# Two-layer retention and convolution trunk on one Trainium2 core: last key tile over 128 rows, TensorE and ScalarE in source order, weight splits one step behind their sums

## Chip, core and metric

The kernel runs on one core of one Trainium2 chip. The metric is the device time of one execution in microseconds (us). Three runs of the kernel before gave 1560.03, 1561.87 and 1566.96; the median is 1561.87. The engines are named PE (TensorE; PEld is its weight load), ACT (ScalarE), DVE (VectorE), POOL (GpSimd) and SP (SyncE, which issues the DMAs).

## What is computed

The reference is a trunk of two layers over 16 + 512 = 528 tokens and 1024 channels. Cut to what matters:

```
for l in range(2):
    xn = rmsnorm(h, pre_norm_g[l])
    proj = xn @ w_in[l] + b_in[l]                # 1024 x 12288
    c_h,c_b,c_c,c_z, r_q,r_k,r_v,r_z, g_a,g_b = split(proj)
    y_a = (c_b * conv3(c_c * c_h) * silu(c_z)) @ w_conv_out[l]
    y_b = (groupnorm(retention(rope(r_q), rope(r_k), r_v)) * silu(r_z)) @ w_ret_out[l]   # 4 heads
    y = (sigmoid(g_a) * y_a + sigmoid(g_b) * y_b) @ w_o[l]
    h = h + rmsnorm(y, post_norm_g[l])
return h[:, 16:]
```

## The kernel before

**Precision.** Every product of a weight and an activation is made of three matmuls on reduced fp32 (fp32r): high part by high part, high by low, low by high. So every weight tile is split: a cast to the high part on ACT (L142) and the difference on DVE (L143), together `split`. Raw weights come by DMA from SP into `raw` tiles; the pairs of split weights are `whi`/`wlo` (four slots) and `whd`/`wld`.

**A Group** (class `Group`) computes 256 output channels for all tokens with seven multiplications of block sums in place of eight (Strassen's scheme). Each multiplication, `mul` (L279), is 12 matmuls of up to 264 columns into one PSUM bank, and between multiplications ACT reads a bank out (`put` at L325, the copy from `pb` to `pa` at L335). In the order of the source these are M1 (bank `pb`, then ACT copies `pb` to `pa`), M5 (`pc`), the pending last multiplication of the group before, S2 (`pb`), A12 (`pa`), S4 (`pc`), S3 (`pb`); the group's own last one, A22, is left in `pending`, accumulates onto the same `pb` bank that S3 used, and is entered by `close()`, either inside the next group or ahead of a `RetOut`. A22 may start only when ACT's `put` has read S3 from that bank. The weights of S2 to S4 and A22 are sums of raw blocks, made on DVE (L307, L314, L315) ahead of their split.

**Between groups** stand `RetOut` (the retention output, L244, two rounds of 48 matmuls; its run begins with `close()`), `ConvOut` (also L244), the retention itself (scores L425, transposes L450, `attend` L484), and at the layer boundary `wo_half`, `norms` and `opening` (L678; norm statistics L370, spread over partitions L384 with ACT's copy L387). The end is the output projection on token rows (L1167) with its own norm (L1183, L1188).

**The retention's last key tile** has 64 keys which lie twice in 128 rows. Its scores are split into `Shi` (128 rows) and `Slo`; in `attend` the pass with `Slo` multiplies the first 64 rows alone.

**What sets the order.** The source calls `tick()` after each multiplication, and `later(n, fn)` puts work n ticks behind; evictions are marked with high priority. A scheduler then orders the instructions of each engine, so a row of PE need not stand where the source has it: it moves matmuls whose inputs are ready in between others. SP, POOL and DVE are ordered in the same way.

Of the kernel before, what the change touches and what calls it, by code (L numbers as in the profile page):

```python
# [11 lines left out]
F32 = mybir.dt.float32  # L12
# [3 lines left out]
ALU = mybir.AluOpType  # L16
# [40 lines left out]
def trunk(ctx: ExitStack, tc: tile.TileContext, xT, w_in, binT, w_co, w_ro, w_o, gpre, gpost,  # L57
# [104 lines left out]
    def load(fn):  # L162
# [3 lines left out]
        return order[0]  # L166

    def prep(kind, need, frees, fn, ready=lambda: True):
        preps.append((kind, need, frees, fn, ready))
# [30 lines left out]
    def pair_of(ref, dram):  # L200

        need = plain_load(ref, dram)

        def go():
            ref["w"] = wtile("whi"), wtile("wlo")
            split(*ref["w"], ref["raw"])
        prep("pair", need, 1, go)
# [76 lines left out]
    class Group:  # L284
        def __init__(self, l, col, i0, cb, act=AF.Identity):
# [6 lines left out]
            prep("one", need[2], 0, self.last)  # L292
            self.raw, self.w = [None] * 3, [None] * 4

# [9 lines left out]
        def halves(self, j):  # L304
            if j != 1:
                r = self.raw[j]
                nc.vector.tensor_tensor(r[:, 512:], r[:, 512:], r[:, 0:512], op=ALU.add)  # L307
            self.w[j] = wtile("whi"), wtile("wlo")
            split(*self.w[j], self.raw[j])

# [7 lines left out]
        def last(self):  # L318
            self.w[3] = tuple(wsd.tile([P, 512], F32R, tag=x, name=nm(x)) for x in ("whd", "wld"))
            split(*self.w[3], self.t4)  # L320

# [5 lines left out]
        def run(self, s1_first=False):  # L327
            l, m, n, w = self.l, self.m, self.n, self.w
            t1, t2, s = fslot(), fslot(), fslot()
            b, c = bank("pb"), bank("pc")  # L330

            def m1():
# [10 lines left out]
            used("pair")  # L343
            close()
            mul(b, S2, w[1], 0, n, False)
            self.put(s, 0, b, scale=-1.0)
            mul(pa, A12, w[1], 1, n, False)
            self.put(t1, 0, pa, self.act)
            used("pair")
            mul(c, S4, w[2], 0, n, False)  # L350
            self.put(t2, 0, c, bias=bias(l, m + 1))
# [5 lines left out]

            def end():
                mul(b, A22, w[3], 0, n, False)
                self.put(t1, 1, b, self.act, bias=bias(l, m))  # L360
# [54 lines left out]
    def scores(l, q, k, k8, Shi, Slo, js):  # L415
# [14 lines left out]
        for n, j, cols in todo:  # L430
# [10 lines left out]
            ss = slice(SOFF[j] + o, SOFF[j] + o + cols.w)  # L441
            later(1, lambda kn=kn, ss=ss, sv=sv: split(Shi[0:kn, ss], Slo[0:kn, ss], sv))

# [22 lines left out]
    def attend(l, h, Shi, Slo, V, v, t, sums):  # L466
# [12 lines left out]
        for n, (j, x, y, b, lo_, hi_) in enumerate(todo):  # L479
            _, kn, q0 = JT[j]  # L480
            if j == len(JT) - 1 and x == 0:
                kn = CHUNK
            S = (Shi, Slo)[y]
# [44 lines left out]
    class RetOut:  # L528
# [4 lines left out]
        def run(self, yr):  # L533
            cols = QCOLS[self.l]
            close()
            for mm in range(2):
                i = self.q * 2 + mm
# [74 lines left out]
    class ConvOut:  # L612
# [6 lines left out]
        def run(self, conv, ga):  # L619
            cols = QCOLS[self.l]  # L620
            cs = slice(cols.t0, T)
            pp = pslot()
            hi, lo = (kview(x, KD) for x in self.ref["w"])
            mm_tile([pp[:, 0, :], pp[:, 1, :]], hi, lo, slice(0, P), lambda k: conv[k][0], lambda k: conv[k][1], KD, cols)
# [147 lines left out]
    def norms(l, half, hts, ysum, hsum, R2, R):  # L772
# [22 lines left out]
        later(2, lambda: tok("y", ysum))  # L795
        later(5, lambda: spread(R2, st["y"], half * HALF, 88, 3))
        for k in range(KD):
            later(5, lambda k=k: resid(k))
        later(13, lambda: tok("h", hsum))
        later(16, lambda: spread(R, st["h"], half * HALF, 88, 3))  # L800
        for k in range(KD):
            later(16, lambda k=k: scaled(k))

# [22 lines left out]
    for l in range(DEPTH):  # L826
# [35 lines left out]
        def q_done(ts, hd, h, l, d=8):  # L862
# [4 lines left out]
            def tables():  # L867
                hd["S"] = [gr.tile([P, SW], F32R, tag="S", name=nm(x), bufs=2) for x in ("Shi", "Slo")]
                nc.sync.dma_start(Dsb, decay[h])
            later(3, tables)  # L870
# [205 lines left out]
    for l in range(DEPTH):  # L1076
# [74 lines left out]
        else:  # L1151
# [62 lines left out]
            for t in range(2, SEQ // P):  # L1214
                st = state()
                for half in range(2):
                    o = pslot()[:, 0, :]
                    for k in range(KD):
# [86 lines left out]
```

## Time and profile before

| | before |
|---|---|
| median of three runs | 1561.87 us |
| profiled execution | 1560.22 us, of which the span 1558.4 us |
| PE busy | 1537.1 us (99%) |
| PEld busy | 1487.0 us (95%) |
| DVE busy | 1166.1 us (75%) |
| ACT busy | 912.2 us (59%) |
| POOL busy | 18.8 us (1%) |
| granted TensorE clock, mean of the span | 1.000 |

Busy time on PE has modelled ends, since matmuls are pipelined. Where PE waits is therefore read from the starts: consecutive matmuls of 264 columns start about 0.12 us apart, and a longer distance between two starts is time lost. The figure in brackets at a row's end is the idle time of the engine ahead of it by the profile, with what ended it.

### The profile page before, as it was taken

What the parts mean: (1) busy time and instruction counts of PE and PEld (TensorE: products, weight loads), DVE (VectorE), ACT (ScalarE), POOL (GpSimd) and SP (SyncE); (2) the same over time, 40 slices, a digit from 0 to 9 for tenths busy, and PEclk for the clock granted to TensorE, in tenths of its full rate; (3) what the DMA queues carried; (4) which work ended last, traced back from release to release, by engine and by line L of the source; (5) the groups of instructions that cost most, each with busy time, mean ns of one, the idle gap of its engine ahead of it and who ended that gap; (6) DMA issues with size and microseconds to landing.
All of it is one profiled execution on the core that took longest, in us unless ns stands there. A gap on an engine that the chain in (4) does not pass through costs nothing.

```text
span 1558.4 us, 29296 instructions
## 1 busy us (share of the span) xinstructions
PE 1537.1 (99%) x11762; PEld 1487.0 (95%) x11762; DVE 1166.1 (75%) x1702; ACT 912.2 (59%) x1763; POOL 18.8 (1%) x23
## 2 busy tenths in 40 slices
PE   9999999999999999999999999999999999999997
PEld 9999999999999999999999999999999999999986
DVE  6997776886878788857367987769778777996642
ACT  6685665565465467646345766655755655776521
POOL 0000000000000000000000000000000000000000
PEclk9999999999999999999999999999999999999999
DMA  8132332232232333435321223322322323334421
GB/s 270 57 128 75 116 109 96 102 110 91 97 106 89 116 122 125 140 129 181 107 104 62 102 95 109 116 98 99 122 95 89 109 97 120 136 131 141 145 88 54
DMA packets 86039, 174.37 MB, mean 112 GB/s; under 512 B 11280, under 2 KB 15888, under 8 KB 85904
## 3 DMA queue, kind: packets, MB, share of 16 engines
q1 hardware_dynamic: 85760, 172.50, 32.0%
q8 instruction: 92, 1.51, 0.4%
q14 instruction: 43, 0.35, 0.1%
q10 hardware_dynamic: 144, 0.01, 0.0%
HBM read 168.21 MB, written 4.26 MB: 111 GB/s over the span
## 4 chain that ended last, share of the span: by engine, by line
PE 91%; DVE 4%; ACT 2%; DMA 1%; issue 1%; SPq 0%; DVEq 0%; POOLq 0%; ACTq 0%
PE pb L279 29%; PE pp L244 18%; PE pc L279 15%; PE pa L279 7%; PE pp L678 7%; PE pp L484 4%; PE pb L678 3%; PE pp L1167 3%; PE pp L425 2%; DMA raw<-in_w_in 1%; PE pp L450 1%; DVE wlo L143 1%; PE pp L384 1%; PE pp L370 1%; ACT whi L142 1%
## 5 line engine op out<-in xcount | busy, mean ns | idle before, releaser
L143 DVE TENSOR_TENSOR wlo<-raw,whi 128x1024 fp32r<-128x1024 f32 (+2 forms) x358 | 394.0, 1109 | 136.9 <-ACT whi L142 135.3
L142 ACT CAST whi<-raw 128x1024 fp32r<-128x1024 f32 (+2 forms) x358 | 339.7, 959 | 251.1 <-PE pp L244 66.2
L279 PE MATMUL pb<-Xh,whi 128*128 128x264 f32 (+2 forms) x1008 | 289.9, 288 | 3.5 <-ACT pa L335 2.3
L279 PE MATMUL pb<-Xh,wlo 128*128 128x264 f32 (+2 forms) x1008 | 285.7, 283 | 0.0
L279 PE MATMUL pb<-Xl,whi 128*128 128x264 f32 (+2 forms) x1008 | 285.4, 283 | 0.0
L244 PE MATMUL pp<-r,whi 128*128 128x264 f32 (+1 forms) x1152 | 246.1, 321 | 0.0
L279 PE MATMUL pc<-Xh,whi 128*128 128x264 f32 (+2 forms) x672 | 193.8, 288 | 1.8 <-ACT f L325 1.5
L279 PEld LDWEIGHTS pb<-Xh,whi 128*128 128x128 f32 x1008 | 189.8, 188 | 5.7 <-ACT pa L335 3.1
L244 PEld LDWEIGHTS pp<-r,whi 128*128 128x128 f32 x1152 | 177.8, 188 | 15.9 <-ACT whi L142 0.3
L279 PE MATMUL pc<-Xl,whi 128*128 128x264 f32 (+2 forms) x672 | 190.7, 284 | 0.0
L279 PEld LDWEIGHTS pb<-Xl,whi 128*128 128x128 f32 x1008 | 189.8, 188 | 0.6
L279 PE MATMUL pc<-Xh,wlo 128*128 128x264 f32 (+2 forms) x672 | 190.3, 283 | 0.0
L279 PEld LDWEIGHTS pb<-Xh,wlo 128*128 128x128 f32 x1008 | 189.8, 188 | 0.0
L244 PE MATMUL pp<-r,wlo 128*128 128x264 f32 (+1 forms) x576 | 153.2, 321 | 0.0
L307 DVE TENSOR_TENSOR raw<-raw 128x512 f32<-128x512 f32 x168 | 115.3, 688 | 27.8 <-DMA raw<-in_w_in 27.0
L279 PEld LDWEIGHTS pc<-Xh,whi 128*128 128x128 f32 x672 | 126.6, 188 | 3.4 <-ACT f L325 2.8
L279 PEld LDWEIGHTS pc<-Xl,whi 128*128 128x128 f32 x672 | 126.6, 188 | 0.1
L279 PEld LDWEIGHTS pc<-Xh,wlo 128*128 128x128 f32 x672 | 126.5, 188 | 0.0
L244 PEld LDWEIGHTS pp<-r,wlo 128*128 128x128 f32 x576 | 95.5, 188 | 7.9
L314 DVE TENSOR_TENSOR raw<-raw,raw 128x512 f32<-128x512 f32 x84 | 58.0, 690 | 57.6 <-DMA raw<-in_w_in 57.4
L279 PE MATMUL pa<-Xh,whi 128*128 128x264 f32 (+2 forms) x336 | 96.8, 288 | 0.0
L279 PE MATMUL pb<-Xh,whd 128*128 128x264 f32 (+2 forms) x336 | 96.3, 287 | 0.3 <-ACT f L325 0.3
(219 smaller groups left out, 3324.0 us busy)
## 6 DMA issues: line engine op xcount, KB each, us to landing
raw<-in_w_in SPq DMA_DIRECT2D x426, 256.0 KB, 2.9
raw<-in_w_ro SPq DMA_DIRECT2D x32, 512.0 KB, 3.2
raw<-in_w_in SPq DMA_DIRECT2D x20, 512.0 KB, 5.0
raw<-in_w_co SPq DMA_DIRECT2D x16, 512.0 KB, 3.2
raw<-in_w_o SPq DMA_DIRECT2D x16, 512.0 KB, 3.8
Dsb<-in_decay SPq DMA_DIRECT2D x8, 520.0 KB, 4.6
h1d<-f SPq DMA_DIRECT2D x8, 264.0 KB, 4.2
f<-h1d SPq DMA_DIRECT2D x8, 264.0 KB, 5.1
```

The source lines that it names most:

```text
L142: nc.scalar.copy(dst_hi, src)
L143: nc.vector.tensor_tensor(dst_lo, src, dst_hi.bitcast(F32), op=ALU.subtract)
L244: nc.tensor.matmul(banks[i][:, 0:cols.n], wt(k)[:, msl], xs(k)[:, sl], start=(k == 0 and a == 0), stop=(k == nk - 1 and a == 2),)
L279: nc.tensor.matmul(o[:, 0:n], wt[:, k, :], xs[:, blk, k, HALF - n:], start=(first and k == 0 and a == 0), stop=(k == 3 and a == 2), skip_g ...
L307: nc.vector.tensor_tensor(r[:, 512:], r[:, 512:], r[:, 0:512], op=ALU.add)
L314: nc.vector.tensor_tensor(b[:, 0:512], a[:, 512:], c[:, 0:512], op=ALU.add)
L370: nc.tensor.matmul(pp[0:sc, 0, c:c + 1], sums[:, t0 + c * sc:t0 + (c + 1) * sc], ones_d[:, 0:1], start=True, stop=True)
L384: nc.tensor.matmul(pp[:, c // per, (c % per) * sc:(c % per + 1) * sc], y[:, c:c + 1].to_broadcast([sc, P]), ident[0:sc, 0:sc], start=True, ...
L425: nc.tensor.matmul(pp[0:kn, n + i, 0:cols.n], k[dt][x][:, k0:k0 + kn] if j < 4 else k8[:, dt * 2 + x, :], q[dt][y][:, sl], start=(dt == 0 ...
L484: nc.tensor.matmul(pp[:, b, lo_ - banks[b][0]:hi_ - banks[b][0]], V[j][x][0:kn, v * P:(v + 1) * P], S[0:kn, SOFF[j] + lo_ - q0:SOFF[j] + h ...
L678: nc.tensor.matmul(o, wt(k), xs[:, i0:], start=(k == 0 and a == 0), stop=(k == KD - 1 and a == 2))
L1167: nc.tensor.matmul(o, x[:, xs], wo[k][half][w], start=(k == 0 and a == 0), stop=(k == KD - 1 and a == 2))
```

## The change

1. The program is opened with a manual schedule for PE and ACT: these two engines issue in the order of the source. DVE, POOL and SP are still ordered by the scheduler.
2. The splits of the weights of a `Group` and of `RetOut`/`ConvOut` are entered by `soon`: one tick after their sums, or at once where the multiplication that needs them comes first (`made[j]()`).
3. `attend` uses all 128 rows for the last key tile. The lower 64 rows of `Slo` there are set to zero by a POOL memset once a head, and the scores' split is written out, with the DVE difference over 64 rows for this tile.
4. In `norms` the delays 5, 13 and 16 become 4, 12 and 14 ticks.
5. In the output projection the two halves of token tile 2 go to the banks `pc` and `pa` in place of a fresh `pp` slot.

```diff
+    def soon(fn):
+        todo = [fn]
+        def now_():
+            if todo:
+                todo.pop()()
+        later(1, now_)
+        return now_
...
-            split(*self.w[j], self.raw[j])
+            self.made[j] = soon(lambda: split(*self.w[j], self.raw[j]))
...
-            split(*self.w[3], self.t4)
+            self.made[3] = soon(lambda: split(*self.w[3], self.t4))
...
+            self.made[0]()
+
             def m1():
...
             close()
+            self.made[1]()
             mul(b, S2, w[1], 0, n, False)
...
+            self.made[2]()
             mul(c, S4, w[2], 0, n, False)
...
             def end():
+                self.made[3]()
                 mul(b, A22, w[3], 0, n, False)
...
-            later(1, lambda kn=kn, ss=ss, sv=sv: split(Shi[0:kn, ss], Slo[0:kn, ss], sv))
+            def halves(kn=kn, ss=ss, sv=sv, n=CHUNK if j == len(JT) - 1 else kn):
+                nc.scalar.copy(Shi[0:kn, ss], sv)
+                nc.vector.tensor_tensor(Slo[0:n, ss], sv[0:n], Shi[0:n, ss].bitcast(F32), op=ALU.subtract)
+            later(1, halves)
...
-            if j == len(JT) - 1 and x == 0:
-                kn = CHUNK
...
             close()
+            self.ref["made"]()
             for mm in range(2):
...
-        later(5, lambda: spread(R2, st["y"], half * HALF, 88, 3))
+        later(4, lambda: spread(R2, st["y"], half * HALF, 88, 3))
...
-        later(13, lambda: tok("h", hsum))
-        later(16, lambda: spread(R, st["h"], half * HALF, 88, 3))
+        later(12, lambda: tok("h", hsum))
+        later(14, lambda: spread(R, st["h"], half * HALF, 88, 3))
...
+                nc.gpsimd.memset(hd["S"][1][CHUNK:, SOFF[4]:].bitcast(F32), 0.0)
                 nc.sync.dma_start(Dsb, decay[h])
...
-                    o = pslot()[:, 0, :]
+                    o = bank(("pc", "pa")[half]) if t == 2 else pslot()[:, 0, :]
...
-    with tile.TileContext(nc) as tc:
+    with tile.TileContext(nc) as tc, tc.manual_schedule(engines={mybir.EngineType.PE, mybir.EngineType.Activation}):
```

**PE at the end of a Group that a RetOut follows** (layer 0, the first such place). `pb` is the group's bank, `whi`/`wlo` its S3 weights, `whd`/`wld` its A22 weights, `pp` and `r` belong to the RetOut. Before:

```order
L279 MATMUL pb_2184<-Xl,whi_2138 128x264
L279 MATMUL pb_2184<-Xh,wlo_2139 128x264
L244 MATMUL pp_2315<-r_1932,whi_2174 128x264 x2
L244 MATMUL pp_2315<-r_1933,whi_2174 128x264 x2
L244 MATMUL pp_2315<-r_1932,wlo_2175 128x264 x2
L244 MATMUL pp_2315<-r_1961,whi_2174 128x264 x2
L244 MATMUL pp_2315<-r_1962,whi_2174 128x264 x2
L244 MATMUL pp_2315<-r_1961,wlo_2175 128x264 x2
L279 MATMUL pb_2184<-Xh,whd_2144 128x264
L279 MATMUL pb_2184<-Xl,whd_2144 128x264
```

The scheduler had set twelve matmuls of the RetOut between S3 and A22. In the changed program (L254 and L289 are L244 and L279 there) none is left:

```order
L289 MATMUL pb_2185<-Xl,whi_2141 128x264
L289 MATMUL pb_2185<-Xh,wlo_2142 128x264
L289 MATMUL pb_2185<-Xh,whd_2145 128x264
L289 MATMUL pb_2185<-Xl,whd_2145 128x264
L289 MATMUL pb_2185<-Xh,wld_2146 128x264
```

The first row of A22 now stands directly behind the last row of S3, on the same bank; before, 16 places of the program had 5 to 12 matmuls between the two, and now 18 have none.

**ACT in the first stage of the program**, where the copies of the first projections (L1018, after: L1038) and the casts of the next weights meet. Before:

```order
L669 ACTIVATE f_396<-YB 128x528
L142 CAST whi_424<-raw_136 128x512
L142 CAST whi_424<-raw_137 128x512
L142 CAST whi_434<-raw_416 128x512
L1018 COPY f_407<-pp_124 128x264 x2
L1018 COPY f_410<-pp_125 128x264 x2
L1018 COPY f_413<-pb_126 128x264
```

After:

```order
L688 ACTIVATE f_398<-YB 128x528
L1038 COPY f_409<-pp_126 128x264 x2
L1038 COPY f_412<-pp_127 128x264 x2
L1038 COPY f_415<-pb_128 128x264
L1038 COPY f_415<-pb_129 128x264
L142 CAST whi_426<-raw_138 128x512
L142 CAST whi_426<-raw_139 128x512
```

The two casts to the first `whi` tile stood ahead of the copies and now stand behind all six of them.

**PE at the second spread of the norm ahead of `opening`'s second half** (L384, after: L399; `ny` holds the norm factors). Before:

```order
L678 MATMUL pb_9982<-Xl,Xh 128x264
L678 MATMUL pb_9982<-Xh,Xl 128x264
L384 MATMUL pp_10087<-ident,ny_10048 128x88 x3
L678 MATMUL pp_10124<-r_9799,whi_9195 128x264
L678 MATMUL pp_10124<-r_9801,whi_9195 128x264
```

After:

```order
L697 MATMUL pb_9988<-Xh,Xl 128x264
L399 MATMUL pp_10069<-ident,ny_10042 128x88 x3
L697 MATMUL pp_9986<-Xh 128x264
L697 MATMUL pp_9986<-Xl,Xh 128x264
L697 MATMUL pp_9986<-Xh,Xl 128x264
L697 MATMUL pb_9987<-Xh 128x264
```

Before, the opening's matmuls on the normed rows (`r`) follow the spread directly; now 24 matmuls that do not need it stand between, and the first one on `r` comes behind them. The first spread, ahead of the opening's first half, moves in the same way from zero to 24 matmuls.

## Rows read from the trace of the kernel before

**Rows 1.** The page: busy time of each engine, and the chain's shares by engine.

```profile
PE 1537.1 (99%) x11762; PEld 1487.0 (95%) x11762; DVE 1166.1 (75%) x1702; ACT 912.2 (59%) x1763; POOL 18.8 (1%) x23
PE 91%; DVE 4%; ACT 2%; DMA 1%; issue 1%; SPq 0%; DVEq 0%; POOLq 0%; ACTq 0%
```

**Rows 2.** Busy time by stretch: PE, PEld, DVE, ACT, POOL, granted clock, DMA share, GB/s.

```profile
40.00:80.00 40.00, 40.00 (x331) 40.00 (x330) 39.88 (x63) 24.78 (x50) 0.00 (x0) 1.00 0.18 62
```

**Rows 3.** Order of time (start, duration): A22 behind RetOut matmuls, PE then ACT.

```profile
177.59 0.40 PE L244 MATMUL pp<-r,wlo 128*128 128x264 f32 x2
177.92 0.39 PE L279 MATMUL pb<-Xh,whd 128*128 128x264 f32 x1
...
176.44 1.05 ACT L142 CAST whi<-raw 128x1024 fp32r<-128x1024 f32 x1 [0.84 <-PE pb L279]
177.40 0.47 ACT L325 ACTIVATE f<-pb,bin 128x264 f32<-128x264 f32 x1
```

**Rows 4.** Order of time: PE at S2 directly behind M1 on one bank.

```profile
496.74 0.28 PE L279 MATMUL pb<-Xh,wlo 128*128 128x264 f32 x1
497.63 0.39 PE L279 MATMUL pb<-Xh,whi 128*128 128x264 f32 x1 [0.60 <-ACT pa L335]
497.86 0.29 PE L279 MATMUL pb<-Xl,whi 128*128 128x264 f32 x1
```

**Rows 5.** The 64-row matmul by form; in order of time; then narrow matmuls of 128 rows.

```profile
L484 PE MATMUL pp<-Slo,r 64*128 64x64 f32 x32 | 9.4, 294 | 0.0
...
114.48 0.29 PE L484 MATMUL pp<-Slo,r 64*128 64x64 f32 x1
114.70 0.39 PE L279 MATMUL pb<-Xh,whd 128*128 128x264 f32 x1
114.93 0.29 PE L279 MATMUL pb<-Xl,whd 128*128 128x264 f32 x1
...
222.40 0.78 PE L425 MATMUL pp<-r,r 128*128 128x64 f32 x6
223.01 0.37 PE L279 MATMUL pc<-Xh,whi 128*128 128x264 f32 x1
223.22 0.28 PE L279 MATMUL pc<-Xl,whi 128*128 128x264 f32 x1
```

**Rows 6.** Order of time, PE at the two spreads of the norm.

```profile
790.89 0.80 PE L384 MATMUL pp<-ident,ny 88*128 88x88 f32 x6
793.40 0.39 PE L678 MATMUL pb<-Xh,whi 128*128 128x264 f32 x1 [1.71 <-ACT Xh L142]
...
818.83 0.80 PE L384 MATMUL pp<-ident,ny 88*128 88x88 f32 x6
821.07 0.39 PE L678 MATMUL pp<-r,whi 128*128 128x264 f32 x1 [1.44 <-ACT r L142]
```

**Rows 7.** Order of time, PE at the third token tile of the output projection.

```profile
1529.93 0.50 PE L1167 MATMUL pp<-Xh,r 128*128 128x512 f32 x1 [1.70 <-DVE z L1188]
```

**Rows 8.** Order of time, PE: a wait for an eviction that stood late.

```profile
937.11 0.28 PE L279 MATMUL pb<-Xh,wlo 128*128 128x264 f32 x1
938.13 0.39 PE L279 MATMUL pc<-Xh,whi 128*128 128x264 f32 x1 [0.73 <-ACT f L325]
```

**Rows 9.** Order of time, first stage: ACT's cast and last two copies, then PE.

```profile
23.57 0.62 ACT L142 CAST whi<-raw 128x512 fp32r<-128x512 f32 x1 [0.46 <-PE pp L678]
25.18 0.70 ACT L1018 COPY f<-pb 128x264 f32<-128x264 f32 x2
...
24.96 0.28 PE L678 MATMUL pp<-Xh,whi 128*128 128x264 f32 x1
```

**Rows 10.** Order of time: the first Group of layer 0 on PE.

```profile
84.17 0.39 PE L279 MATMUL pb<-Xh,whi 128*128 128x264 f32 x1 [1.15 <-ACT f L1026]
```

**Rows 11.** Order of time: the split ahead of a RetOut, ACT then DVE.

```profile
504.78 1.06 ACT L142 CAST whi<-raw 128x1024 fp32r<-128x1024 f32 x1 [0.23 <-PE pp L244]
505.87 1.23 DVE L143 TENSOR_TENSOR wlo<-raw,whi 128x1024 fp32r<-128x1024 f32 x1
```

More of the change, by code (lines that the diff above doesn't have):

```diff
@@ L205, in go @@
             ref["w"] = wtile("whi"), wtile("wlo")
-            split(*ref["w"], ref["raw"])
+            ref["made"] = soon(lambda: split(*ref["w"], ref["raw"]))
         prep("pair", need, 1, go)
@@ L292, in __init__ @@
             prep("one", need[2], 0, self.last)
-            self.raw, self.w = [None] * 3, [None] * 4
+            self.raw, self.w, self.made = [None] * 3, [None] * 4, [None] * 4
         def load(self, j, w):
@@ L622, in run @@
             pp = pslot()
+            self.ref["made"]()
             hi, lo = (kview(x, KD) for x in self.ref["w"])
@@ L795, in norms @@
         later(2, lambda: tok("y", ysum))
-        later(5, lambda: spread(R2, st["y"], half * HALF, 88, 3))
+        later(4, lambda: spread(R2, st["y"], half * HALF, 88, 3))
         for k in range(KD):
-            later(5, lambda k=k: resid(k))
-        later(13, lambda: tok("h", hsum))
-        later(16, lambda: spread(R, st["h"], half * HALF, 88, 3))
+            later(4, lambda k=k: resid(k))
+        later(12, lambda: tok("h", hsum))
+        later(14, lambda: spread(R, st["h"], half * HALF, 88, 3))
         for k in range(KD):
-            later(16, lambda k=k: scaled(k))
+            later(14, lambda k=k: scaled(k))
     def opening(tiles, half, ts):
```

## Prediction

> **What bounds the kernel now.** I read the page first: PE is busy for 1537 of 1558 us, DVE for 75%, ACT for 59%, and the chain that ended last runs on PE for 91% [rows 1]. So the time is the sum of the distances between matmul starts, and only three things can move it: fewer or cheaper matmuls, PE waits that go, and PE waits that come. The granted clock is 1.00 in the stretch shown and in the mean of the span [rows 2], so nothing is to be had there. The waits come next, read in order of time: a matmul of 264 columns starts 0.12 us after the one before it, and what is beyond that is lost. The page's own count of PE's idle time is 1558 minus 1537, 21 us [rows 1], so 1.4% is all that better order alone could give; the starts show where it lies: almost none in the middle of a layer's steady run, most where stages meet. The last view is the busy time by stretch: from 40 to 80 us DVE is busy for 39.88 of 40 us [rows 2], which is the one stage where a late DVE result could hold ACT.
>
> **What the change takes away.**
>
> *64-row matmuls.* There are 32 of them [rows 5]. The one at 114.48 takes 0.22 us to the next start and the matmul behind it 0.23, together 0.45. Six narrow matmuls of 128 rows take 0.61 us to the next start, 0.10 each, and the one behind them 0.21, together 0.31 [rows 5]. The difference is 0.14; the narrow `Shi` matmul ahead loses some 0.03 too. So I take 0.17 x 32 = 5.3 us off, with 0.10 and 0.25 as ends (3.2 to 8.1: the upper if both neighbours fall to the plain 0.12). The eight memsets go to POOL, which is busy for 18.8 us in all [rows 1], and the DVE and ACT halves of the split stay as long as they were: no cost. If POOL were late, `attend` would wait, but the memset stands a whole score stage ahead of it.
>
> The Trainium skill speaks against this gain: the page "TensorE: Matmul & The Clock Gate", section "Why this matters for your kernels", says that a single matmul with few rows takes the same time as one with 128, since what counts is the columns. By that rule the term is 0. The rows here differ by row count at equal columns, 0.22 against 0.10, so I go by the rows; the rule has its case below.
>
> *Norms.* PE waits behind the two spreads: from 790.89 to 793.40 and from 818.83 to 821.07, in which six narrow matmuls need some 0.6 us each time [rows 6]. That leaves 1.9 and 1.6, and 0.3 more at the second DVE half of the first row tile: 3.9 us. In the new order 24 matmuls (24 x 0.12 = 2.9 us) stand between spread and first use, against a chain of 2.24 and 2.51 us from the first spread matmul to the first use [rows 6]. All of it goes: 3.9, with 3.0 as the lower end.
>
> *Third token tile.* PE is idle for 1.70 us at 1529.93 till DVE has read the old bank [rows 7]; banks `pc` and `pa` are long free then. With the late restart seen in [rows 4]: 1.8 off.
>
> *Late evictions.* Between 98.89 and 938.13 us there are six waits for an eviction that the scheduler had set behind casts; the last one loses 1.02 minus 0.12 and 0.1 at the restart, 1.0 [rows 8]. Together 3.7. In source order, with casts one step behind, the put stands first. I take 3.7, ends 2 and 4.3.
>
> Sum of gains: 5.3 + 3.9 + 1.8 + 3.7 = 14.7 us (9.9 to 18).
>
> **What it brings.**
>
> *S3 to A22.* This is the largest term. A22 adds onto the bank that ACT must first read for S3. Before, up to twelve RetOut matmuls, up to 1.45 us, lay between: there the loss was 0.2 us, because a cast of 1.05 us stood ahead of the put [rows 3]. Now 18 places have nothing between them. The same dependence with nothing between is in the trace, S2 behind M1: 0.89 us between starts instead of 0.12, so 0.77, and 0.11 at the restart, 0.88 [rows 4]. Whether the restart is paid depends on A22's weights being loaded ahead; I take 0.82. Three places in layer 1 have a put in two pieces, 0.2 more each. 18 x 0.82 + 0.6 = 15.4, minus the 2.0 that before loses at eight of these places (the first is [rows 3]): +13.4, ends 12.5 and 15. ACT has nothing else queued ahead of these puts: the cast now stands one multiplication earlier or behind.
>
> *First Group of layer 1.* M1 is followed directly by S2 in this one Group: one more wait like [rows 4], +0.9.
>
> *RetOut behind c_z.* Two RetOuts follow each other with one pair of slots; the second one's cast (1.06) and difference (1.23) start when the first is done [rows 11]. Before, some multiplications were moved in between and 2.6 us were lost over both layers; now nothing is. About 2.15 a layer, 4.3 in all: +1.7, ends 0.5 and 3.
>
> *First stage.* The casts to the first `whi` tile stood ahead of the copies; PE used it from 24.96 on. Now they follow six copies, which end at 25.88, and one cast takes 0.5 to 0.6 [rows 9]. The matmul waits till about 26.4, 1.5 us, and 0.4 more for the low half: +1.9, ends 1 and 2.5.
>
> *First Group of layer 0.* The wait for L1026 at 84.17 [rows 10] goes, but the splits of this Group's inputs now stand behind four scalings and DVE is full just there [rows 2]: M1 waits till 86 or 87. Net +2, ends 0 and 3.
>
> *Small ones.* Two norm statistics are read by DVE with no matmul moved between (2 x 0.4, half of a wait like [rows 4], since what is read is a few columns) and the transposes at the end wait a little more: +1.3.
>
> Sum of losses: 13.4 + 0.9 + 1.7 + 1.9 + 2 + 1.3 = 21.2 us (16 to 25).
>
> Net +6.5 us on the profiled 1560.2, so 1566.7 there. The median is 1.7 above the profiled execution, and I keep that distance: **1568.4 us**, 0.4% longer. A difference of 0.5% (7.8 us) is about what a measurement of this kernel can tell from none, so the forecast is "the same", near the slower edge. By the ends of the terms the case reaches from 1561 to 1575.
>
> **Rivals.**
>
> *ACT in source order holds the evictions (slower).* A cast waits for a DVE sum; behind it on ACT stands the put that PE waits for. In source order nothing overtakes it. It decides from the point where a sum is later than the put's input, by more than the room that a put has in the steady run: two multiplications of 1.45 us between its input and its reader's next use of the bank, against a put of 0.47 and up to two casts of 1.05 [rows 3], some 0.4 us. DVE is full from 40 to 80 us [rows 2] and nearly so to 130, and a Group lasts about 10 us; if the five Groups there and as many at the score stages of the other heads each lose one cast of 1.05 us [rows 3], that is 10 more: 1579. For it speaks the full DVE; against it that the casts now stand a step behind their sums, which gives DVE 1.45 us more.
>
> *The row count does not matter (slower).* The 0.22 us of the 64-row matmul would then come from its place at the end of a chain, not from its rows, and would stay: 5.3 us are lost from the gains, 1573.7. This is the rule of the Trainium skill's page "TensorE: Matmul & The Clock Gate" named above; [rows 5] speak against it.
>
> *The wait at A22 is short (faster).* If the put starts earlier than behind M1 and PE's queue hides most of it, the 18 places cost 0.2 us each as in [rows 3], 3.6 minus 2.0 in place of 13.4, and the total is 1556.6; with the upper end of the 64-row term 1553.8. For it: A22's weights lie ready long before. Against: the read of the bank alone takes 0.47 us [rows 3], and it can't start before S3's last matmul ends.
>
> *The change does not reorder what it says.* The new order of both engines shows the places named, so only a small chance is left: then the terms that don't depend on order remain, 64 rows and the third tile, 7.1 off: 1554.8.
>
> **How the numbers follow.** Forecast 0.60, evictions held 0.15, row count 0.07, short wait 0.13, no reordering 0.05. Within the forecast's range of 1561 to 1575 some 0.37 of the 0.60 lie below 1569.7. Slower: 0.23 + 0.15 + 0.05 = 0.43, with 0.02 of the row-count case below the edge; same: 0.37 + 0.02 + 0.11 = 0.50 with the larger part of the short wait and of the last case; faster: the remaining 0.07. The range leaves out the far ends of both sides: 1556 to 1577.
>
> **What would show it.** In the trace of the changed kernel the first A22 matmul behind S3 starts 0.8 to 0.9 us after S3's last one, 18 times, with ACT's put (L335 there) as releaser. The narrow `Slo` matmuls are 128 rows and 0.10 to 0.12 us apart. No wait stands behind L399 and none at the third token tile. ACT's first `whi` cast of 512 columns stands behind six copies at 25.9. I am wrong if puts stand behind casts that wait for DVE, if the 18 waits are under 0.4, or if PE's narrow matmuls keep their 0.22. A granted clock under 1.00 in any middle stretch would be a cause that no term here holds.

## The result, and the profile after

The changed kernel takes 1609.59 us in the median (1607.88 to 1612.51); the kernel before took 1561.74 in the same comparison. The ratio is 1.0303, 95% interval 1.0274 to 1.0331: 3% slower, some 48 us. The forecast was 1568.4 with a range up to 1577. No rival reached this either.

The page of the changed kernel has the same work in it and less of it covered:

```profile
PE 1548.9 (96%) x11762; PEld 1496.2 (93%) x11762; DVE 1169.4 (73%) x1702; ACT 901.5 (56%) x1763; POOL 22.7 (1%) x31
PE 84%; DVE 8%; ACT 5%; issue 1%; DMA 1%; DVEq 0%; SPq 0%; POOLq 0%; ACTq 0%
```

The span is 1607.9 us instead of 1558.4. The matmuls are as many as before, but PE is now idle for 59 us (1607.9 minus 1548.9) where [rows 1] left 21, and the chain that ended last runs on PE for 84% where it ran for 91%: 8% of it is DVE and 5% ACT. So PE waits for the other two. Of the 49.5 us by which the span grew, 37.7 are idle time of PE; the other 11.8 are longer busy time for as many matmuls, which goes with a lower granted clock (below). For whom PE waits, its waits say (what waited, for whom; us in total, times, longest):

```profile
PE pb L289 <- ACT f L335: 23.9, 22, 3.1
PE pp L697 <- ACT f L839: 6.9, 2, 3.4
PE pp L254 <- DVE wlo L143: 3.8, 4, 1.8
PE pc L289 <- ACT f L335: 3.7, 8, 0.9
PE pb L289 <- ACT Xh L142: 2.0, 1, 2.0
PE pb L289 <- DVE Xl L143: 1.7, 1, 1.7
```

L335 is `put` now, L839 the opening's eviction, L254 RetOut, L289 `mul`. Before, all waits for `put` and the copy to `pa` together were 4.1 us; here those for `put` alone are 27.6. Of the 22 waits in the first row, 18 are A22 behind S3, 19.1 us together.

Where the 49.5 us of the span came from, by the start of the matmul with the same number in both traces (11,762 in each):

| stage of the changed kernel | us more than before |
|---|---|
| first stage, to 44 us | +3.0 |
| first Group of layer 0 (wait at 88) | +4.0 |
| the wait for DVE near 138 us, which is gone | -2.4 |
| convolution product of layer 0 (wait at 161) | +3.3 |
| heads 1 to 3 of layer 0 | +4.2 |
| third conv Group and its RetOuts, 505 to 530 | +8.4 |
| the rest of layer 0 | +1.0 |
| layer boundary: norms and opening, 807 to 880 | +11.5 |
| first Group of layer 1 | +1.4 |
| heads of layer 1 | +6.2 |
| third conv Group and its RetOuts, 1300 to 1334 | +7.8 |
| the rest, the third token tile included | +1.1 |

**The waits that were forecast are there.** At the first A22 behind S3 (PE, then ACT, in order of time: start, duration):

```profile
184.13 0.29 PE L289 MATMUL pb<-Xh,wlo 128*128 128x264 f32 x1
184.98 0.39 PE L289 MATMUL pb<-Xh,whd 128*128 128x264 f32 x1 [0.57 <-ACT f L335]
...
184.45 0.48 ACT L335 ACTIVATE f<-pb,bin 128x264 f32<-128x264 f32 x1 [0.97 <-PE pb L289]
```

From 184.13 to 184.98 are 0.85 us, 0.73 beyond the normal distance, and the restart adds 0.11 to 0.12: 0.85, near the 0.88 of [rows 4] for S2. This is the price at eleven of the 18 places (0.83 to 0.85); at one more, with a put in two pieces, it is 0.99.

**The other six are dearer, because ACT gets to the put late.** At the third place, ACT:

```profile
289.69 0.63 ACT L142 CAST r<-f 128x528 fp32r<-128x528 f32 x1 [0.81 <-DVE f L535]
290.23 1.04 ACT L142 CAST whi<-raw 128x1024 fp32r<-128x1024 f32 x1
291.18 0.47 ACT L335 ACTIVATE f<-pc,bin 128x264 f32<-128x264 f32 x1
291.55 0.62 ACT L142 CAST r<-f 128x528 fp32r<-128x528 f32 x1
292.07 0.48 ACT L335 ACTIVATE f<-pb,bin 128x264 f32<-128x264 f32 x1
```

The put at 292.07 was due at about 291.2. A cast of the retention's output (`r`) had waited for its DVE product (L535), and a weight cast, the put of S4 and another `r` cast stood in line behind it. PE lost 1.73 us here, and 3.35 at the place behind the third conv Group (510 us). The longest of this kind is at the convolution product:

```profile
159.99 0.63 ACT L142 CAST r<-f 128x528 fp32r<-128x528 f32 x1 [1.74 <-DVE f L616]
160.53 0.38 ACT L335 ACTIVATE f<-pb 128x264 f32<-128x264 f32 x1
...
160.96 0.59 PE L289 MATMUL pb<-Xh,whi 128*128 128x264 f32 x1 [2.71 <-ACT f L335]
```

ACT stands idle for 1.74 us on a DVE product with PE's eviction behind it.

At the layer boundary it is the opening's evictions (L839) that come late. ACT at the second and the third of three places:

```profile
847.13 0.82 ACT L142 CAST Xh<-YB 128x264 fp32r<-128x264 f32 x2 [1.03 <-DVE YB L810]
847.86 0.85 ACT L839 ACTIVATE f<-pp,bin 128x264 f32<-128x264 f32 x2
...
860.32 4.26 ACT L142 CAST whi<-raw 128x512 fp32r<-128x512 f32 x8 [10.88 <-PE pp L697]
864.49 2.19 ACT L839 ACTIVATE f<-pp,bin 128x8 f32<-128x8 f32 x8
```

PE waits 1.25 us at 832, 3.42 at 849 and 3.43 at 866. What stands ahead of the evictions differs: at 832 the squares for the norm (L688), which wait for DVE; at 849 casts of the normed rows, which wait for DVE; at 866 eight casts of the next weights, 4.26 us of work.

**Behind a long wait the matmuls run at half the rate.** PE at the opening's second half:

```profile
845.06 0.28 PE L697 MATMUL pp<-r,wlo 128*128 128x264 f32 x1
848.76 0.52 PE L697 MATMUL pp<-r,whi 128*128 128x264 f32 x2 [3.42 <-ACT f L839]
...
849.23 0.41 PE L697 MATMUL pp<-r,whi 128*128 128x264 f32 x2
...
849.60 0.40 PE L697 MATMUL pp<-r,whi 128*128 128x264 f32 x2
...
850.56 0.64 PE L697 MATMUL pp<-r,whi 128*128 128x264 f32 x2
...
851.22 0.64 PE L697 MATMUL pp<-r,whi 128*128 128x264 f32 x2
...
853.56 0.29 PE L697 MATMUL pp<-r,wlo 128*128 128x264 f32 x1
853.68 0.41 PE L697 MATMUL pp<-r,whi 128*128 128x264 f32 x2
```

Up to 850 three matmuls take 0.37 us (849.23 to 849.60), from 850.56 on they take 0.66 (to 851.22), 0.22 each instead of 0.12, and from 853.56 on 0.12 again. The stretches (busy PE, PEld, DVE, ACT, POOL; then granted clock, DMA share, GB/s) show it as the clock, whose mean falls where the lower of its two levels (1.2 in place of 2.4 GHz) is granted for a part of the stretch:

```profile
840.00:855.00 15.00, 11.58 (x83) 11.37 (x82) 6.23 (x16) 5.12 (x13) 0.00 (x0) 0.89 0.00 1
855.00:870.00 15.00, 11.57 (x84) 11.35 (x83) 9.03 (x15) 6.36 (x16) 0.00 (x0) 0.90 0.35 122
500.00:520.00 20.00, 14.63 (x103) 14.00 (x103) 17.27 (x27) 10.42 (x18) 0.00 (x0) 0.91 0.21 72
```

The same happens at seven places in the middle of this trace, behind the waits at 88, 161, 510, 818, 849, 866 and 1307 us; the means of the stretches around them are 0.83 to 0.93. That makes some 27 us at the lower level, and up to 13 us of lost time if PE had work throughout (an estimate from those means). The trace of the kernel before has no such place (mean 1.000; other executions of it have means down to 0.994).

### The profile page after: what moved, and what is told of

Its sections match the earlier page's. It is cut to its first block, busy times and chain, and to the rows that moved or that the text cites. A ratio compares the mean times of both kernels' runs of the same rounds, so it can differ in the third digit from the quotient of the medians.

```text
span 1607.9 us, 28953 instructions
## 1 busy us (share of the span) xinstructions
PE 1548.9 (96%) x11762; PEld 1496.2 (93%) x11762; DVE 1169.4 (73%) x1702; ACT 901.5 (56%) x1763; POOL 22.7 (1%) x31
## 3 DMA queue, kind: packets, MB, share of 16 engines
HBM read 168.21 MB, written 4.26 MB: 107 GB/s over the span
## 4 chain that ended last, share of the span: by engine, by line
PE 84%; DVE 8%; ACT 5%; issue 1%; DMA 1%; DVEq 0%; SPq 0%; POOLq 0%; ACTq 0%
PE pb L289 27%; PE pp L254 17%; PE pc L289 14%; PE pa L289 7%; PE pp L697 5%; PE pp L501 5%; PE pp L440 2%; PE pp L1187 2%; DVE wlo L143 2%; PE pb L697 2%; ACT whi L142 1%; DVE r L143 1%; PE pp L469 1%; ACT f L335 1%; DVE f L535 1%
## 5 line engine op out<-in xcount | busy, mean ns | idle before, releaser
L142 ACT CAST whi<-raw 128x1024 fp32r<-128x1024 f32 (+2 forms) x358 | 337.6, 955 | 98.9 <-PE pp L254 79.3
L289 PE MATMUL pb<-Xh,whi 128*128 128x264 f32 (+2 forms) x1008 | 290.5, 288 | 7.8 <-ACT f L335 4.8
L289 PE MATMUL pb<-Xl,whi 128*128 128x264 f32 (+2 forms) x1008 | 286.3, 284 | 1.7 <-DVE Xl L143 1.7
L289 PE MATMUL pb<-Xh,wlo 128*128 128x264 f32 (+2 forms) x1008 | 286.4, 284 | 0.0
L254 PE MATMUL pp<-r,whi 128*128 128x264 f32 (+1 forms) x1152 | 247.0, 323 | 1.8 <-ACT whi L142 1.8
L289 PEld LDWEIGHTS pb<-Xh,whi 128*128 128x128 f32 x1008 | 190.9, 189 | 9.7 <-ACT f L335 5.7
L289 PE MATMUL pc<-Xh,whi 128*128 128x264 f32 (+2 forms) x672 | 193.8, 288 | 3.7 <-ACT f L335 3.7
L254 PEld LDWEIGHTS pp<-r,whi 128*128 128x128 f32 x1152 | 179.2, 190 | 18.3 <-ACT whi L142 2.4
L289 PEld LDWEIGHTS pb<-Xl,whi 128*128 128x128 f32 x1008 | 190.9, 189 | 2.3 <-DVE Xl L143 1.9
L289 PEld LDWEIGHTS pb<-Xh,wlo 128*128 128x128 f32 x1008 | 190.7, 189 | 0.0
L289 PE MATMUL pc<-Xl,whi 128*128 128x264 f32 (+2 forms) x672 | 190.4, 283 | 0.0
L289 PE MATMUL pc<-Xh,wlo 128*128 128x264 f32 (+2 forms) x672 | 190.1, 283 | 0.0
L254 PE MATMUL pp<-r,wlo 128*128 128x264 f32 (+1 forms) x576 | 154.6, 323 | 3.8 <-DVE wlo L143 3.8
L289 PEld LDWEIGHTS pc<-Xh,whi 128*128 128x128 f32 x672 | 126.5, 188 | 6.7 <-ACT f L335 6.3
L289 PEld LDWEIGHTS pc<-Xl,whi 128*128 128x128 f32 x672 | 126.5, 188 | 0.0
L289 PEld LDWEIGHTS pc<-Xh,wlo 128*128 128x128 f32 x672 | 126.3, 188 | 0.0
L335 ACT ACTIVATE f<-pb,bin 128x264 f32<-128x264 f32 (+2 forms) x186 | 83.3, 458 | 60.5 <-PE pb L289 56.1
L289 PE MATMUL pb<-Xh,whd 128*128 128x264 f32 (+2 forms) x336 | 97.4, 290 | 19.1 <-ACT f L335 19.1
L254 PEld LDWEIGHTS pp<-r,wlo 128*128 128x128 f32 x576 | 96.2, 189 | 13.8 <-DVE wlo L143 5.4
L289 PE MATMUL pa<-Xh,whi 128*128 128x264 f32 (+2 forms) x336 | 96.4, 287 | 0.0
```

Source lines behind the costliest of these rows:

```text
L142: nc.scalar.copy(dst_hi, src)
L254: nc.tensor.matmul(banks[i][:, 0:cols.n], wt(k)[:, msl], xs(k)[:, sl], start=(k == 0 and a == 0), stop=(k == nk - 1 and a == 2),)
L289: nc.tensor.matmul(o[:, 0:n], wt[:, k, :], xs[:, blk, k, HALF - n:], start=(first and k == 0 and a == 0), stop=(k == 3 and a == 2), skip_g ...
L335: nc.scalar.activation(dst[:, t0:t0 + c1 - c0], o[:, c0 - self.i0:c1 - self.i0], func, **kw)
```

## The experiments

I began with this theory: PE's own order costs the 18 waits and no more; the rest is ACT, which in source order lets casts that wait for DVE stand ahead of puts. The rival: the loss is PE's order itself.

### Scheduler back on, all other edits kept

```diff
-    with tile.TileContext(nc) as tc, tc.manual_schedule(engines={mybir.EngineType.PE, mybir.EngineType.Activation}):
+    with tile.TileContext(nc) as tc:
```

> The changed kernel without the manual schedule: PE and ACT ordered by the scheduler again, all other edits kept. Theory H (evictions held on ACT, whose source order lets casts that wait for DVE stand ahead of puts): nearly all of the 48 us goes back, and the 128-row tile and the third token tile still give their 5 and 2 us: 1550 to 1560. Rival S (the splits one step behind their sums cost time by themselves): stays above 1575. The A22 multiplications have RetOut matmuls ahead of them again, so the 18 waits of 0.8 us go in either case.

Measured: 1550.04 us, ratio 0.9918 (0.9901 to 0.9936), 12.8 us faster than before. Everything that was lost, and more, hangs on the manual schedule. The other edits are a gain.

### Only PE, and only ACT in source order

```diff
+    ... tc.manual_schedule(engines={mybir.EngineType.PE}):
```

> The changed kernel with only PE in source order; ACT is ordered by the scheduler. Theory H: puts may stand ahead of casts again, so what remains is the 18 waits of A22 behind S3 at 0.8 to 0.9 us each, some 14 us over the kernel with both engines scheduled: 1563 to 1575, granted clock 1.00. Rival P (the loss comes from PE's source order, which leaves PE nothing to do while a bank is read): it stays at 1595 to 1610.

Measured: 1595.42, ratio 1.0204 (1.0189 to 1.0220).

```diff
+    ... tc.manual_schedule(engines={mybir.EngineType.Activation}):
```

> The changed kernel with only ACT in source order; PE is ordered by the scheduler. Theory H: the long waits stay (88, 161, 510, 848, 866 and 1307 us in the changed kernel), those of A22 behind S3 shrink, since 12 of 16 places have matmuls between again: 1585 to 1600, and the granted clock falls under 0.95 in the same stretches. Rival P: 1555 to 1568.

Measured: 1557.85, ratio 0.9965 (0.9954 to 0.9977), clock 0.999.

My theory fell with these two. ACT's source order alone costs 0.5% (0.9965 against 0.9918), 7 us; PE's alone costs 2.9%, 45 us; both cost 3.9%, 60 us. At the place of the convolution product ACT is held in just the same way with only ACT in source order:

```profile
153.98 0.63 ACT L142 CAST r<-f 128x528 fp32r<-128x528 f32 x1 [1.74 <-DVE f L616]
154.52 0.38 ACT L335 ACTIVATE f<-pb 128x264 f32<-128x264 f32 x1
...
154.95 0.39 PE L289 MATMUL pb<-Xh,whi 128*128 128x264 f32 x1 [1.45 <-ACT f L335]
```

ACT waits the same 1.74 us. PE loses 1.45 us here and 1.46 at its next wait for a put (158.13 us), together 2.9, where the changed kernel lost 2.71 in one piece: at this place the matmuls that the scheduler put in between divide the wait and do not save it. No lower clock follows here: it is 1.00 from 150 to 165 us, and 0.89 in the changed kernel.

That a held eviction can cost nothing is shown at the layer boundary. ACT with everything scheduled, then ACT and PE with only PE in source order:

```profile
827.37 4.27 ACT L142 CAST whi<-raw 128x512 fp32r<-128x512 f32 x8 [7.12 <-PE pp L697]
831.54 2.18 ACT L839 ACTIVATE f<-pp,bin 128x8 f32<-128x8 f32 x8
...
845.97 4.26 ACT L142 CAST whi<-raw 128x512 fp32r<-128x512 f32 x8 [7.20 <-PE pp L697]
850.14 2.18 ACT L839 ACTIVATE f<-pp,bin 128x8 f32<-128x8 f32 x8
...
851.33 0.51 PE L697 MATMUL pp<-r,Xh 128*128 128x264 f32 x2 [3.45 <-ACT f L839]
```

The same eight casts stand ahead of the evictions in both. With everything scheduled PE has no wait for them; in source order it waits 3.45 us. The squares at 832 behave in the same way (1.25 us, and none). Only the wait at 849 goes when ACT alone is scheduled.

Nor is PE's order innocent where ACT is scheduled. With only PE in source order, PE and ACT at the first A22:

```profile
178.18 0.29 PE L289 MATMUL pb<-Xh,wlo 128*128 128x264 f32 x1
179.86 0.39 PE L289 MATMUL pb<-Xh,whd 128*128 128x264 f32 x1 [1.39 <-ACT f L335]
...
178.38 1.04 ACT L142 CAST whi<-raw 128x1024 fp32r<-128x1024 f32 x1 [0.84 <-PE pb L289]
179.33 0.47 ACT L335 ACTIVATE f<-pb,bin 128x264 f32<-128x264 f32 x1
```

The scheduler sets a cast of 1.04 us ahead of the put, exactly as in [rows 3], but the RetOut matmuls that covered it there are gone: 1.68 us between the starts.

### The 128-row tile alone

```diff
-            if j == len(JT) - 1 and x == 0:
-                kn = CHUNK
...
+                nc.gpsimd.memset(hd["S"][1][CHUNK:, SOFF[4]:].bitcast(F32), 0.0)
```

> The kernel before with the 128-row last key tile alone. By the rows of before: 32 x 0.17 = 5.3 us less, 1556 to 1557, and the Slo matmuls 0.10 to 0.12 us from start to start. By the rule that the row count does not matter: no change, 1562.

Measured: ratio 0.9975 (0.9964 to 0.9986), 2.2 to 5.6 us less than before, 3.9 in the middle. PE at the place of [rows 5], before (the `Shi` row ahead of it), then with the edit:

```profile
114.22 0.33 PE L484 MATMUL pp<-Shi,r 128*128 128x192 f32 x2
...
114.98 0.33 PE L486 MATMUL pp<-Shi,r 128*128 128x192 f32 x2
115.14 0.28 PE L486 MATMUL pp<-Slo,r 128*128 128x64 f32 x1
115.26 0.37 PE L279 MATMUL pb<-Xh,whd 128*128 128x264 f32 x1
115.46 0.28 PE L279 MATMUL pb<-Xl,whd 128*128 128x264 f32 x1
```

From `Shi` to the second matmul of the Group there are 0.48 us where there were 0.71 (114.22, the start of that `Shi` row before, to 114.93): 0.23 for each of 32, 7.4 us, near the upper end, and the other 31 places differ by 0.22 to 0.23 as well. Part of it went into another wait, of L370 for DVE near 138 us: 2.8 us where it was 1.7 before, and 1.5 us more are lost behind it at the lower rate.

### RetOut matmuls ahead of A22, in source order

```diff
-            close()
             self.ref["made"]()
             for mm in range(2):
...
-                        lambda k: yr[k][0], lambda k: yr[k][1], 4, cols)
+                        lambda k: yr[k][0], lambda k: yr[k][1], 4, cols, None if mm else close)
```

`mm_tile` calls `close` after its second input block, so 12 matmuls (6 of 512 columns in layer 1) stand ahead of A22.

> The changed kernel, both engines in source order, but RetOut enters its first 12 (layer 0) or 6 (layer 1) matmuls ahead of the pending A22 multiplication, as the scheduler had done: 16 of the 18 places are filled again. Theory P (PE's source order leaves it nothing to do while ACT reads the bank): the 18 waits, 23.9 us in the changed kernel, shrink to some 7, and one or two clock dips behind them go: 17 to 20 us less, 1589 to 1593. Rival (the waits only move to the next late result): under 6 us less, above 1603.

Measured: 1601.06, ratio 1.0227 (1.0210 to 1.0244): 12 us less than the changed kernel (1.0303), between the two expectations. The waits of `pb` for `put` fell from 23.9 to 6.5 us, those at the A22 places among them from 19.1 to 1.1, so theory P has its mechanism, but behind the third conv Group PE then waits for the RetOut's own weights:

```profile
PE pp L254 <- ACT whi L142: 9.8, 4, 4.0
```

It was 1.8 us in the changed kernel. One wait took another's place.

### Splits at their sums again, in source order

```diff
-        later(1, now_)
-        return now_
+        now_()
+        return now_
```

> The changed kernel with the splits of weights entered at their sums again, both engines in source order. If the step behind the sums is what keeps ACT's source order bearable, casts now wait on ACT for sums that DVE has only just been given, with puts behind them: slower than the changed kernel by 10 to 40 us. If it is of no use: 1605 to 1613.

Measured: 1598.95, ratio 1.0221 (1.0206 to 1.0237): 13 us faster than the changed kernel. Both expectations missed. I had the step behind the sums as what spares ACT; it is part of what holds it. A cast entered one multiplication later stands ahead of a later put. Without the step the `pb` waits for `put` fall to 15.3 us, all six A22 places of the heads of layer 0 are back at 0.84 to 0.85, the waits at the seven score stages (0.37 to 0.45 us each) are gone, and the wait at 161 us costs 0.76 in place of 4.33, of which 2.87 were the wait and the rest the lower rate behind it.

### Casts of products on POOL

```diff
+    def split_off(dst_hi, dst_lo, src):
+        nc.gpsimd.tensor_copy(dst_hi, src)
+        nc.vector.tensor_tensor(dst_lo, src, dst_hi.bitcast(F32), op=ALU.subtract)
```

It replaces `split` for the retention output and the convolution product.

> The changed kernel with the casts of the retention output and of the convolution product (48 casts of 528 or 512 columns, which wait for a DVE product) on POOL in place of ACT. Theory H2 (within source order these casts hold the puts behind them): the waits at 161, 292, 400, 505, 510, 1096, 1200 and 1307 us fall to 0.8 or less, with the clock dips behind the two long ones, 13 to 18 us less: 1591 to 1597. Rival: DVE itself is late there, whatever stands on ACT, and the waits stay: 1605 to 1612.

Measured: 1606.49, ratio 1.0271 (1.0256 to 1.0286): 5 us less, not 13 to 18. The held puts are freed (the place at 292 us costs 0.84 there, that at 161 us under 0.6), so the casts did hold them. The place at 292 us is cured by this edit and by the one before it, each alone: its put is late only where the product cast and the weight cast entered late stand ahead of it together. But at the third conv Group the wait only changes its name:

```profile
PE pp L258 <- DVE wlo L143: 10.0, 4, 4.7
```

This is again RetOut's weights (L258 there), 3.8 us in the changed kernel.

### Matmuls that nobody reads, in four long waits

```diff
+            if self.h == H - 1 and not self.q:
+                heat(pslot()[:, 0, 0:HALF], 24)
             close()
...
+            if half:
+                heat(bank("pc")[:, 0:HALF], 24)
```

> The changed kernel with 24 matmuls that nobody reads (2.9 us at 0.12) ahead of four long waits: at A22 behind the third conv Group (510 and 1307 us) and at both steps of the opening's second half (848 and 866 us). The waits end when they did. If the lower granted clock behind them follows from PE's having been idle, the matmuls behind them keep 0.12 us and 1.5 to 2 us go at each place: 1602 to 1604. If the clock falls for another reason: 1608 to 1612.

Measured: ratio 1.0257 (1.0242 to 1.0272), 7 us less than the changed kernel at the same work plus 96 matmuls. The opening's stretches are at the full clock, that at 510 us is not:

```profile
840.00:855.00 15.00, 14.49 (x119) 14.28 (x118) 6.22 (x16) 4.96 (x13) 0.00 (x0) 1.00 0.00 1
855.00:870.00 15.00, 14.44 (x119) 14.23 (x118) 12.23 (x20) 6.36 (x16) 0.00 (x0) 1.00 0.35 123
500.00:520.00 20.00, 17.24 (x123) 16.39 (x121) 17.21 (x28) 9.79 (x18) 0.00 (x0) 0.91 0.19 66
```

So at the two opening places the lower rate follows from PE's having stood idle. By the starts of the same matmuls in both traces it costs 1.5 us at each of the two, over and above the wait. At 1307 us the clock stays 1.00 too, but PE then waits 2.34 us for RetOut's `wlo` in place of 1.02, and nothing is gained. At 510 us nothing is gained either: behind the filled wait stands another of 1.76 us, which was not filled, and the clock falls as before. So the four places give 3.1 of the 5.9 us between the two profiled spans; the rest lies at places that this edit does not touch, and the 7 us of the medians are not the price of four clock drops.

### Three of the edits on the kernel before

```diff
-                    o = pslot()[:, 0, :]
+                    o = bank(("pc", "pa")[half]) if t == 2 else pslot()[:, 0, :]
...
-        later(16, lambda: spread(R, st["h"], half * HALF, 88, 3))
+        later(14, lambda: spread(R, st["h"], half * HALF, 88, 3))
```

(with the 128-row tile and the other norm delays)

> The kernel before, ordered by the scheduler, with three of the edits: last key tile over 128 rows, token tile 2 on its own banks, and the norm delays. By the waits that the first of these experiments lost (4 us at the norms, 2 us at the token tile) and 4 to 5 us for the rows: 10 to 11 us less than before, ratio 0.993 to 0.994. If the splits one step behind their sums bring something under the scheduler too, this one stays above that kernel's 0.992; if they cost there, it is under it.

Measured: ratio 0.9926 (0.9913 to 0.9938), as expected. Under the scheduler no effect of the step behind the sums is seen (0.9918 with it; the intervals overlap).

### The old norm delays, in source order

```diff
-        later(14, lambda: spread(R, st["h"], half * HALF, 88, 3))
+        later(16, lambda: spread(R, st["h"], half * HALF, 88, 3))
```

> The changed kernel with the norm delays of before (5, 13, 16). If the earlier spreads bring their 4 us under the source order as well, this is 2 to 5 us slower than the changed kernel: 1611 to 1615, ratio 1.032 to 1.034. If they set the casts of the normed rows ahead of the opening's evictions on ACT, and PE waits for that (848 and 866 us), it is 5 to 8 us faster: ratio 1.025 to 1.027.

Measured: ratio 1.0354 (1.0340 to 1.0368), 8 us slower than the changed kernel. The earlier spreads help in either order, here more than I thought.

### Two costs taken out together, then a third

First both edits from above in one kernel, the splits at their sums and the RetOut matmuls ahead of A22:

> The changed kernel with two of its costs taken out together: splits entered at their sums, and RetOut matmuls ahead of A22. Each alone brought some 12 us. If they are separate costs, 22 to 26 us less than the changed kernel, ratio 1.014 to 1.016; if both removed the same waits, 13 to 16 us, ratio 1.020 to 1.022. What is left over before would then lie at the first Group, the opening and the RetOut pair.

Measured: ratio 1.0160 (1.0144 to 1.0175). The two nearly add up: 22 us (12 and 13 alone). Of what is left, two waits at the RetOuts behind the third conv Group are the largest, 8.0 and 8.7 us by the starts, the lower clock behind them included (497 and 1285 us):

```profile
497.34 0.87 PE L254 MATMUL pp<-r,whi 128*128 128x264 f32 x3 [3.06 <-ACT whi L142]
```

The weights of the fourth conv Group are loaded and split ahead of those RetOuts, though used after them: the list of a conv block's four Groups is built before its RetOuts. They hold three of the four slots for split pairs, and both RetOuts share the last one.

```diff
-        return [Group(l, C_H + i2 * 256, I_CONV[l], c_h), Group(l, C_C + i2 * 256, I_CONV[l], c_c),
+        return (Group(*a) for a in ((l, C_H + i2 * 256, I_CONV[l], c_h), (l, C_C + i2 * 256, I_CONV[l], c_c),
...
```

> The kernel of the last experiment (both engines in source order, splits at their sums, RetOut matmuls ahead of A22), and the weights of the first two RetOuts behind the third conv Group are loaded and split ahead of the fourth Group's, in the order of their use, so that both have a pair of their own. If the 8.0 and 8.7 us that PE waits there come from the place of these splits, 14 to 17 us go: ratio 1.005 to 1.007. If they come from DVE's being late at this stage, under 5 us go: 1.013 or more. What stays over before is then the opening and the first Groups of both layers.

Measured: 1572.33, ratio 1.0049 (1.0030 to 1.0068), 17 us less. Of the two waits none is left in layer 0 and 1.2 us in layer 1, and the largest that stay are those of the other stages:

```profile
PE pp L698 <- ACT f L840: 6.9, 2, 3.5
PE pb L291 <- ACT f L337: 3.6, 6, 0.9
PE pb L291 <- ACT Xh L142: 3.1, 1, 3.1
```

L840 is the opening's eviction, L142 here the first Group of layer 0. These were not taken out one by one.

## Why the prediction was wrong

The step that failed is the pricing of the waits: each place was priced as one read of a bank, with ACT and DVE taken to be on time ("ACT has nothing else queued ahead of these puts", "the put stands first", "All of it goes"). The runs show evictions that stand late on ACT, and a PE in source order with nothing in line meanwhile: 37.7 us more idle time of PE, and some 12 us lost to a lower clock behind the long waits. Term by term:

**What bounds the kernel** was read rightly: PE, with the waits where stages meet. The conclusion drawn from 21 us of idle time was half of the truth: it bounds what a better order can give, not what a worse one can take.

**64-row matmuls: right in kind, too small.** 5.3 us was the term; the starts show 0.23 x 32 = 7.4 us, of which 3.9 (2.2 to 5.6) reached the time when it was done alone. The Trainium skill's page "TensorE: Matmul & The Clock Gate", section "Why this matters for your kernels", says that a single matmul with few rows takes the same time as one with 128. In this chain, among matmuls of 128 rows, it does not hold: 0.22 us to the next start with 64 rows, 0.11 with 128.

**Norms and third token tile: right under the scheduler.** There the norms' stage is 3.8 us shorter than before and the token tile's 1.9, by the starts of the matmuls with the same number; 3.9 and 1.8 were forecast. In source order the token tile still gave 1.8. At the layer boundary the gain was swamped. The two waits that were priced did go, but PE now waits 1.25, 3.42 and 3.43 us for the opening's evictions (L839) at 832, 849 and 866 us and 2.24 for a norm sum of DVE (`ysum`, 818 us), with the lower clock behind three of the four. The step that failed is "All of it goes": I followed the first user of the spread and not the evictions. Two of them (832, 866) are late on ACT under the scheduler too and cost nothing there, so PE's order makes them dear; the waits at 818 and 849 are absent with only PE in source order. The boundary cost 11.5 us instead of giving 3.9.

**Late evictions: wrong.** The step failed at its reason, "in source order, with casts one step behind, the put stands first". It does not. New losses of 0.62 to 0.70 us came at seven score stages, where a weight cast (1.05 us, at 235.93) and the cast of `whd` (0.61) stand ahead of the put of S4 (237.40), and the one at 161 us cost 3.3. The experiment with the splits at their sums puts 13 us on that half sentence, the late puts of the next term included.

**S3 to A22: right in kind, too small.** 15.4 us were forecast for 18 places; by the starts they cost 23.8. Eleven have the forecast price, one with a put in two pieces 0.99, six have a late put on top. The failed step is "ACT has nothing else queued ahead of these puts". I looked at the weight casts alone and not at the casts of the products, which wait for DVE; together they make the put late.

**RetOut behind the third conv Group: right place, wrong size.** A net +1.7 us was forecast for both layers, and the stage cost 16.2 (8.4 and 7.8), A22's late put there included. The cast and the difference of the second RetOut were priced; that both RetOuts wait, since the next Group's weights hold three slots, was not seen. Changing the load order brought 17 us on top of two other repairs, in a kernel where these waits had grown; what it brings alone was not run.

**First stage and first Groups.** +1.9 was forecast for the first stage and +3.0 came, +2 (0 to 3) for the first Group of layer 0 and +4.0 came, with the lower clock behind its waits of 2.0 and 1.7 us (2.4 us came back later, as the wait near 138 us went), +0.9 for that of layer 1 and 1.4 came.

**The clock was left out.** The forecast said that no term holds a lower granted clock and named it as a sign of error. PE's long waits brought it: the mean is 0.990 in the changed kernel, PE's busy time grew by 11.8 us for as many matmuls, and at two places filling the wait gave 1.5 us each. This alone is more than the whole forecast change.

**The rivals.** The slower one, ACT's order holding the evictions, names the right mechanism and has the wrong places: not the stage where DVE is full, but the score stages, the third conv Groups and the layer boundary, and casts of products as well as of weights. It gave 1579 because each loss was one cast; and it took PE's order as given. Only the runs with one engine each show that PE's order is what makes a held eviction dear: with PE scheduled, 7 us, with PE in source order 15 (1.0303 against 1.0204). By the starts of the same matmuls, 9 of these 15 lie at the layer boundary and 4 at the third conv Group of layer 0; from 170 to 500 us the kernel with only PE in source order is no faster than the changed one. And DVE's order, which the scheduler still sets, differs between these two kernels (some 1,180 of 1,702 rows stand elsewhere), so the 15 us are not ACT's order alone. Between the changed kernel and the one with only ACT in source order ACT's order is the same and DVE's nearly so (145 rows): the 52 us between these two go with PE's order. The faster rivals fell at the eighteen waits, which are 0.85 us and more, and the one on the row count at the 0.23 us.

What stays open: the shares of the opening and of the first Groups within what the last kernel still loses over the scheduled one (1.0049 against 0.9918). Its waits name them, but no run took them out.

The version that beats both kernels is the one with all edits but the manual schedule: 1550.04 us, ratio 0.9918.

## What to carry to other kernels

An order that interleaves two streams of matmuls can cover the round trips through a bank, those that show in no wait of the trace included; when such an order is given up, the price is not the one wait that is seen: it takes in every late result that the other stream had covered. Before an engine is set to source order, list for each of its waiting instructions what stands behind it, product casts as well as weight casts, and ask who has other work in line. And a split that is entered later is not out of the way: it is ahead of something else.

## What the runs showed of the hardware

After PE stood idle for 3.4 us (845.3 to 848.8), its matmuls started 0.12 us apart for another 1.4 us, then 0.22 us apart up to about 853.4, then 0.12 again. The granted clock was 1.00 in the wait itself (845.0 to 848.7) and 0.51 from 850.5 to 853.5: the drop came behind the restart, not with the wait. Where unread matmuls filled the wait but for 0.5 us, the clock was 1.00 in the same stretch; at 510 us, where a second wait of 1.76 us stayed, it fell all the same.

A matmul of 64 rows among matmuls of 128 rows took 0.22 us to the next start and the same one over 128 rows 0.11, and the matmuls beside it lost time too: 0.23 us at each of 32 places.
